# A two-layer diffusion trunk in float32: one float32 matmul per product in place of three float32r matmuls

## The chip, the cores and the metric

The kernel runs on one core of one Trainium2 chip. The metric is the device time of one execution in microseconds (us); lower is better. Such a core has a matrix engine (TensorE, PE in the profile; its weight loads stand apart as PEld), a vector engine (VectorE, DVE), an activation engine (ScalarE, ACT), GpSimd (POOL) and a queue that starts transfers (SyncE, SP). TensorE reads two operands from on-chip memory, a stationary one (`lhsT`, "the weights" of one matmul) and a moving one (`rhs`), and adds its results up in PSUM banks.

## The reference

One step of a trunk of two layers on 384 tokens: 128 of a prompt, 256 of a sample. The same weights serve both. Everything is float32.

```python
def _layer(x, cond, lw, rope, ctx):
    mod = (silu(cond) @ lw['w_mod'] + lw['b_mod'])          # 9 vectors of 1024 per condition
    def pre(j, t):
        return _rmsnorm(t, lw['norm_g'][j]) * (1.0 + mod[3*j+1]) + mod[3*j]
    x = x + 0.5 * mod[2] * _swiglu(pre(0, x), ffn_in[0], ffn_out[0])     # 1024 -> 2*2816 -> 1024
    y, new_ctx = _mixer(pre(1, x), lw, rope, ctx)
    x = x + mod[5] * y
    x = x + 0.5 * mod[8] * _swiglu(pre(2, x), ffn_in[1], ffn_out[1])
    return x, new_ctx
```

The mixer multiplies its input with `w_in` (1024 x 5888), runs three branches (attention of 8 heads with 2 key heads, a gated linear recurrence of 4 heads in both directions called HGRN2, and attention within a window), multiplies each with a 512 x 1024 matrix, gates and adds them, and multiplies with `w_out` (1024 x 1024). The outputs are the tokens after a last norm, the prompt's keys and values, and the recurrence's states.

## The kernel before

Activations lie with features on the 128 partitions and the 384 tokens along the row, as eight tiles `xt[k]`. A weight matrix comes from HBM in chunks of at most 128 x 1024 float32 (512 KB), each of which holds up to eight 128 x 128 blocks. A product of one block with one activation tile is called a product here: it adds 128 out features x 384 tokens into a PSUM bank.

Each product is three matmuls (`mm3`, line 211). The type float32r is a float32 that TensorE takes with a rounded mantissa; a number is split into an upper float32r part and the rest as a lower one. `wchunk` (line 194) loads a chunk into a tile `wr` (4 buffers), casts it on ScalarE to `wh` (line 200) and subtracts that on VectorE for `wl` (line 201). `split` (line 204) does the same with activations (`ah`/`al`, `oh`/`ol`, `mh`/`ml`); `norm_tile` makes `hh`/`hl`, `residual` makes `xh`/`xl`, `key_parts` and `query_parts` the parts for the scores of attention (`kh`, `kl`, `kpr`, `kpl`, `qst`). `mm3` adds upper x upper, upper x lower and lower x upper.

The order of the work: a start in which the first modulation vectors come on TensorE (`mod_start`, with 32-column matmuls on `condS`, then four 2-column ones against `sel`); then for each layer a SwiGLU (`ffn`), the mixer, and a second SwiGLU. A SwiGLU has a first group of six out tiles with the k tiles outermost (`first_group`, 48 products), 19 pairs of out tiles of eight products each per tile (304), and eight out tiles of 22 products (176). The mixer has a first group (48), 24 products of 256 columns for the values, 40 tiles of eight (320), two token-major pieces of 24 products with 512 columns (`by_token`), the three branch matrices (96) and `w_out` (64). In layer 0 the first group of the first SwiGLU has 384 columns, the five other first groups have 386.

Attention, HGRN2 and the other modulation vectors (`mods`: tiles `wm` of 512 KB, two reductions on VectorE each, line 236) are side work, written as generators. `side.pump` is called after each chunk with the nominal time of its products and lets each generator go on by its rate. `UN` is this nominal time for one product; `ATR`, `HGR` and `MMX` set the rates. So the program text sets which side work stands between which products. A tool of the language then orders the instructions for each engine by priority; each engine runs its own in that order, and waits by semaphores.

These matmuls are plain float32 in both kernels: the sums of squares against `ones`, broadcasts against `ident`, attention's transposes and weighted sums (`weigh`), everything in `hg_head`, and the head norms of the queries in `q_norms` (line 836), which go to four groups of 32 columns of TensorE, one for each of the four query tiles:

```python
for j, x in enumerate(xs):
    sq = block("sq")
    A.activation(sq, x, AF.Square)
    mm(p[32 * j:32 * j + 32], bd32, sq, True, True)
```

Of the kernel before, what the change touches and what calls it, by code (L numbers as in the profile page):

```python
# [9 lines left out]
F32 = mybir.dt.float32  # L10
F32R = mybir.dt.float32r
# [19 lines left out]
AHEAD = 60  # L31
MMX = 320.0
NBLK = 60
NWH = 4
NWL = 4
NWR = 4
URG = 100
HGR = 2.0
ATR = 2.4
# [4 lines left out]
def tile_trunk(ctx: ExitStack, tc: tile.TileContext, ins: dict, outs: dict, depth=DEPTH):  # L44
# [63 lines left out]
    # silu(cond), features on the partitions: 32 columns, of which two count  # L108
# [30 lines left out]
    def lower_bounds():  # L139
        """softmax over the layers, cumulated, less the first"""  # L140
# [63 lines left out]
    def split(src, name):  # L204
        hi = block(name + "h", F32R)
        lo = block(name + "l", F32R)
        A.copy(hi, src)  # L207
        V.tensor_tensor(lo, src, hi, ALU.subtract)  # L208
        return hi, lo

    def mm3(out, w, x, start, stop):
        mm(out, w[0], x[0], start, False)
        mm(out, w[0], x[1], False, False)
        mm(out, w[1], x[0], False, stop)

    def wslice(c, i):
        return c[0][:, i * P:(i + 1) * P], c[1][:, i * P:(i + 1) * P]
# [21 lines left out]
    def start_tile(tag):  # L239
        return wp.tile([P, 1024], F32, tag=tag, bufs=3 if tag == "wm" else NWL, name=nm("st"))  # L240

    def mod_start_load(g):
        ws = []
        for q, tag in enumerate(("wm", "tok", "wm", "wl")):
# [36 lines left out]
    def mods(*ljs):  # L281
        """loads run one tile ahead of the sums"""
# [41 lines left out]
    def rstd_bcast(ps_cols, n, width):  # L324
        """rows of sums (token-major) -> 1/sqrt(mean + eps), small tile"""
# [8 lines left out]
    def norm_scale(state, copy=True):  # L334
        """1 / sqrt(mean + eps) of every token, on all partitions"""
# [11 lines left out]
    def norm_tile(bc, l, j, k):  # L347
        if True:
            t = block("t")
            for c, a, b in CONDS:  # L350
                V.scalar_tensor_tensor(t[:, a:b], xt[k][:, a:b], mcol(l, 3 * j + 1, k, c), bc[:, a:b],  # L351
                                       ALU.mult, ALU.mult)
            hi = block("hh", F32R)
            lo = block("hl", F32R)
            for c, a, b in CONDS:
                sh = mcol(l, 3 * j, k, c)
                A.activation(hi[:, a:b], t[:, a:b], AF.Identity, bias=sh)  # L357
                V.scalar_tensor_tensor(lo[:, a:b], t[:, a:b], sh, hi[:, a:b], ALU.add, ALU.subtract)
            return hi, lo

    def group_part(name, l, ps, xs, kp, raws=None):
        cs = [wchunk(ins[name][l, kp, e], 768, raws[2 * kp + e] if raws else None) for e in range(2)]
        for kk in range(2):
            k = 2 * kp + kk
            for e in range(2):
                for q in range(3):
                    mm3(ps[3 * e + q], wslice(cs[e], 2 * q + kk), xs[k], k == 0, k == KT - 1)
# [17 lines left out]
    def group_scale(p, bcs):  # L385
        """the scale of the norm on a product, and the products of the shifts"""
# [7 lines left out]
    def residual(state, n, ps, l, j, nxt):  # L394
# [4 lines left out]
        if nxt is not None:  # L399
            l2, j2 = nxt  # L400
            hi = block("xh", F32R, T + 2)
            lo = block("xl", F32R, T + 2)
            for c, a, b in CONDS:
                gs = mcol(l2, 3 * j2 + 1, n, c)
                A.activation(hi[:, a:b], xt[n][:, a:b], AF.Copy, scale=gs)
                V.scalar_tensor_tensor(lo[:, a:b], xt[n][:, a:b], gs, hi[:, a:b], ALU.mult, ALU.subtract)
            sh = modt[l2][:, 24 * j2 + n]
            A.copy(hi[:, T:T + 2], sh)
            V.tensor_tensor(lo[:, T:T + 2], sh, hi[:, T:T + 2], ALU.subtract)
            state["xs"].append((hi, lo))  # L410
        sumsq_add(state, xt[n])

# [1 line left out]
    def ffn(state, l, i, nxt, mhid=(), mout=(), start=None):  # L414
        acts = []

        def finish_pair(pg, pu):
# [4 lines left out]
            acts.append(split(s, "a"))  # L422
# [8 lines left out]
        else:  # L431
# [3 lines left out]
            for j in range(first):  # L435
# [5 lines left out]
                acts.append(split(tu, "a"))  # L441
        for j in range(first, FT):
            pair = []
            for w in range(2):
                c = pre.pop(0) if pre else wchunk(ins["wfi"][l, i, j, w], 1024)
                p = pside() if j == first else pmain()
                for k in range(KT):
                    mm3(p, wslice(c, k), hs[k], k == 0, k == KT - 1)
# [6 lines left out]
            if j == first:  # L455
                tm = side.add(mods(*mhid), (8 * len(mhid) + 1) / 128.0)
# [3 lines left out]
        tm = side.add(mods(*mout), (8 * len(mout) + 1) / 62.0)  # L460
        for n in range(KT):
            p = pmain()
            for q, (a, b) in enumerate(((0, 8), (8, 15), (15, 22))):
                c = wchunk(ins["wfo"][l, i, n][:, a * P:b * P], (b - a) * P)
                for k in range(a, b):
                    mm3(p, wslice(c, k - a), acts[k], k == 0, k == FT - 1)
# [7 lines left out]
    def rope(dst, src, tmp):  # L474
        """dst = src * cos + swapped(src) * sin on the sample's columns"""
# [7 lines left out]
    def key_parts(keys, kp):  # L483
        """float32r parts of the keys of both kv heads: the upper part of a head on both halves of the partitions,
        the lower part too; the prompt's keys apart"""
        res = []
        pr = block("kpr", F32R).rearrange("p (a b) -> p a b", a=3)
        pl = block("kpl", F32R).rearrange("p (a b) -> p a b", a=3)
        for g in range(2):
            kh, kl = block("kh", F32R), block("kl", F32R)  # L490
            own, oth = slice(64 * g, 64 * g + 64), slice(64 - 64 * g, 128 - 64 * g)
            for src, h, lo in ((keys, kh, kl), (kp, pr[:, g], pl[:, g])):
                A.copy(h[own], src[own])
                A.copy(h[oth], src[own])
                V.tensor_tensor(lo[own], src[own], h[own], ALU.subtract)
                V.tensor_tensor(lo[oth], src[own], h[own], ALU.subtract)
            res.append((kh, kl, pr[:, g], pl[:, g]))
        return res

    def query_parts(qt, hf):  # L500
        """[upper; lower] float32r parts of one head on the halves of the partitions"""
        st = block("qst", F32R)
        own, oth = slice(64 * hf, 64 * hf + 64), slice(64 - 64 * hf, 128 - 64 * hf)
        A.copy(st[own], qt[own])
        V.tensor_tensor(st[oth], qt[own], st[own], ALU.subtract)
        return st

    def scores(l, win, j, hf, st, ks, rq):
        hidx = 4 * hf + j
        kh, kl, ph, pl = ks[hf]  # L510
# [45 lines left out]
    def weigh(pts, vs):  # L556
        """the heads of a pair take turns: each has one half of the columns of TensorE"""
# [9 lines left out]
    def attn_task(specs):  # L567
        """specs: (layer, win, q tiles, key parts, scales of q, values, result); heads overlap by one"""
        work = [(sp, j, hf) for sp in specs for j in range(4) for hf in range(2)]
        parts = {}  # L570

        def prepare(w):
# [604 lines left out]
```

## Time and profile before

| | before |
|---|---|
| median of 3 runs | 1965.35 us (1963.71 to 1965.65) |
| profiled execution, first to last instruction (span) | 1962.9 us |
| what lies around it (median less span) | 2.45 us |
| TensorE busy | 1943.3 us, 11958 matmul records |
| VectorE busy | 1445.4 us |
| ScalarE busy | 903.6 us |
| moved by DMA | 303.81 MB, 155 GB/s over the span |

The profiled execution's own total is not listed apart; its span is what its rows add up to. A record is one instruction that the profiler saw on an engine. Matmul records overlap: the engine streams the columns of the next one while the results of the last one still drain, and the end of a record is modelled. So what one matmul costs in a stream is the distance from start to start, not the duration of its record.

### The profile page before, as it was taken

Reading aid. Unit: us, or ns where it says so; the run is one execution under the profiler, and the core shown is the slowest. Engines: PE = TensorE matmul, PEld = TensorE weight load, DVE = VectorE, ACT = ScalarE, POOL = GpSimd, SP = SyncE. Lnnn points to the kernel's source line nnn. Section 1 sums busy time; section 2 is a strip of 40 time slices with the busy share of each in tenths; the row PEclk is TensorE's granted clock in tenths of the full one; section 3 lists DMA queues with packets and bytes.
Section 4 is the critical chain, followed back from the end, with each engine's and each line's share of the span. In section 5 each row is a group of like instructions: output and inputs, shape, how many; then the busy total and the mean of one; then the engine's idle time right before and its main releaser. Section 6 shows DMA issues by size and latency. Waiting matters only on the chain.

```text
span 1962.9 us, 31192 instructions
## 1 busy us (share of the span) xinstructions
PE 1943.3 (99%) x11958; PEld 1878.0 (96%) x11958; DVE 1445.4 (74%) x2945; ACT 903.6 (46%) x1764; POOL 13.2 (1%) x28
## 2 busy tenths in 40 slices
PE   7999999999999999999999999999999999999998
PEld 4999999998999999999999999998989999999998
DVE  4697876878888689866579869588878867765433
ACT  4433334665555454333353333356655545533331
POOL 0000000000000000000000000000000000000000
PEclk8999999999999999999999999999999999999999
DMA  7775653422334347655447657443213334444441
GB/s 277 247 254 193 226 195 121 134 87 76 113 114 135 124 139 235 216 190 177 141 157 238 222 184 251 124 132 108 86 55 114 97 104 145 151 161 156 122 126 64
DMA packets 94517, 303.81 MB, mean 155 GB/s; under 512 B 11936, under 2 KB 16416, under 8 KB 94368
## 3 DMA queue, kind: packets, MB, share of 16 engines
q1 hardware_dynamic: 93600, 300.25, 46.7%
q8 instruction: 94, 1.54, 0.3%
q0 software_dynamic: 768, 1.57, 0.2%
q14 instruction: 55, 0.45, 0.1%
HBM read 298.63 MB, written 3.15 MB: 154 GB/s over the span
## 4 chain that ended last, share of the span: by engine, by line
PE 98%; DMA 1%; DVE 0%; SPq 0%; ACT 0%; issue 0%; DVEq 0%
PE pm L82 83%; PE ps L82 14%; PE ps L548 1%; DMA st<-in_wst 0%; DMA wr<-in_wfg 0%; SPq L88 0%; DVE y L1068 0%; PE ps L549 0%; PE ps L775 0%; PE ps L715 0%; PE ps L714 0%; ACT wh L200 0%; DVE x L397 0%; PE ps L842 0%; ACT sq L303 0%
## 5 line engine op out<-in xcount | busy, mean ns | idle before, releaser
L200 ACT CAST wh<-wr 128x1024 fp32r<-128x1024 f32 (+3 forms) x460 | 444.6, 967 | 802.7 <-PE pm L82 414.1
L201 DVE TENSOR_TENSOR wl<-wr,wh 128x1024 fp32r<-128x1024 f32 (+3 forms) x460 | 513.8, 1119 | 210.8 <-ACT wh L200 205.3
L82 PE MATMUL pm<-hh,wh 128*128 128x384 f32 x1816 | 617.4, 340 | 0.0
L82 PE MATMUL pm<-hl,wh 128*128 128x384 f32 x1816 | 613.8, 338 | 0.0
L82 PE MATMUL pm<-hh,wl 128*128 128x384 f32 x1816 | 611.7, 337 | 0.0
L236 DVE CUSTOM_DVE_ANT_0 junk<-wm,cond 128x1024 bf16<-128x1024 f32 x256 | 312.7, 1222 | 55.7 <-DMA wm<-in_wmod 49.9
L82 PEld LDWEIGHTS pm<-hh,wh 128*128 128x128 f32 x1816 | 340.8, 188 | 6.8 <-issue 3.1
L82 PEld LDWEIGHTS pm<-hl,wh 128*128 128x128 f32 x1816 | 341.1, 188 | 1.9 <-DVE t L351 0.8
L82 PEld LDWEIGHTS pm<-hh,wl 128*128 128x128 f32 x1816 | 341.5, 188 | 1.4 <-issue 1.4
L82 PE MATMUL pm<-al,wh 128*128 128x384 f32 x704 | 237.3, 337 | 0.0
L82 PE MATMUL pm<-ah,wl 128*128 128x384 f32 x704 | 237.0, 337 | 0.0
L82 PE MATMUL pm<-ah,wh 128*128 128x384 f32 x704 | 237.0, 337 | 0.0
L82 PEld LDWEIGHTS pm<-al,wh 128*128 128x128 f32 x704 | 132.3, 188 | 0.0
L82 PEld LDWEIGHTS pm<-ah,wl 128*128 128x128 f32 x704 | 132.2, 188 | 0.0
L82 PEld LDWEIGHTS pm<-ah,wh 128*128 128x128 f32 x704 | 132.1, 188 | 0.0
L397 DVE SCALAR_TENSOR_TENSOR x<-pm,modt,x 128x128 f32<-128x128 f32 x96 | 35.5, 412 | 56.7 <-PE pm L82 56.6
L421 DVE TENSOR_TENSOR silu<-pm,silu 128x384 f32<-128x384 f32 x73 | 40.5, 555 | 48.0 <-PE pm L82 47.6
L207 ACT CAST ah<-silu 128x384 fp32r<-128x384 f32 x79 | 40.4, 512 | 35.4 <-DVE silu L421 35.0
L357 ACT ACTIVATE hh<-t,modt 128x128 fp32r<-128x128 f32 x96 | 42.4, 454 | 29.8 <-DVE t L351 29.6
L82 PE MATMUL pm<-oh,wh 128*128 128x384 f32 x128 | 46.2, 361 | 0.0
L208 DVE TENSOR_TENSOR al<-silu,ah 128x384 fp32r<-128x384 f32 x79 | 43.5, 551 | 1.5 <-ACT ah L207 1.5
L351 DVE SCALAR_TENSOR_TENSOR t<-x,modt,bcs 128x128 f32<-128x128 f32 x96 | 37.1, 412 | 10.1 <-ACT bcs L344 10.0
(306 smaller groups left out, 2737.4 us busy)
## 6 DMA issues: line engine op xcount, KB each, us to landing
wr<-in_wfi SPq DMA_DIRECT2D x152, 512.0 KB, 3.8
wm<-in_wmod SPq DMA_DIRECT2D x128, 512.0 KB, 4.6
wr<-in_win SPq DMA_DIRECT2D x80, 512.0 KB, 3.7
wr<-in_wfo SPq DMA_DIRECT2D x64, 448.0 KB, 3.4
wr<-in_wfo SPq DMA_DIRECT2D x32, 512.0 KB, 3.6
wr<-in_wfg SPq DMA_DIRECT2D x32, 384.0 KB, 3.1
wr<-in_wbr SPq DMA_DIRECT2D x48, 256.0 KB, 2.6
st<-in_wst SPq DMA_DIRECT2D x16, 512.0 KB, 7.0
```

The costliest lines, as they stand in the source:

```text
L82: PE.matmul(out, lhsT=lhsT, rhs=rhs, start=start, stop=stop)
L200: A.copy(hi, raw)
L201: V.tensor_tensor(lo, raw, hi, ALU.subtract)
L207: A.copy(hi, src)
L208: V.tensor_tensor(lo, src, hi, ALU.subtract)
L236: V.tensor_tensor_reduce(junk, w, cond[c], 1.0, 0.0, ALU.mult, ALU.add, accum_out=modt[l][:, n, c:c + 1])
L351: V.scalar_tensor_tensor(t[:, a:b], xt[k][:, a:b], mcol(l, 3 * j + 1, k, c), bc[:, a:b], ALU.mult, ALU.mult)
L357: A.activation(hi[:, a:b], t[:, a:b], AF.Identity, bias=sh)
L397: V.scalar_tensor_tensor(xt[n][:, a:b], ps[:, a:b], mcol(l, j, n, c), xt[n][:, a:b], ALU.mult, ALU.add)
L421: V.tensor_tensor(s, pu, s, ALU.mult)
L548: PE.transpose(dst, pb[1 + b][:, kt * P:(kt + 1) * P], ident)
```

## The change

`mm3` is gone: each product is one `mm` on the float32 tile `wr` as it came from HBM and on float32 activations. `wchunk` only loads; the casts, the subtractions, `split`, `key_parts` and `query_parts` are gone with their tiles. Behind `weigh` one copy from PSUM remains (`o`). The scores of a head are products on the 64 partitions of that head, three per head in place of six. The pool sizes are `NWR` = 14 buffers for `wr` (4 before, beside 4 each for `wh` and `wl`) and `NBLK` = 52 (60). The nominal time and the rates of the side work change, and modulation vectors 6 and 7 (in layer 1 also 5) move from the SwiGLU to the mixer.

```diff
-AHEAD = 60
-MMX = 320.0
-NBLK = 60
-NWH = 4
-NWL = 4
-NWR = 4
+MMX = 150.0
+NBLK = 52
+NWR = 14
-HGR = 2.0
-ATR = 2.4
+HGR = 1.5
+ATR = 1.55
...
-    def wchunk(src, cols, raw=None):
-        if raw is None:
-            raw = wraw(src, cols)
-        hi = wp.tile([P, 1024], F32R, tag="wh", bufs=NWH, name=nm("wh"))[:, :cols]
-        lo = wp.tile([P, 1024], F32R, tag="wl", bufs=NWL, name=nm("wl"))[:, :cols]
-        with tc.high_priority(offset=AHEAD):
-            A.copy(hi, raw)
-            V.tensor_tensor(lo, raw, hi, ALU.subtract)
-        return hi, lo
...
-    def mm3(out, w, x, start, stop):
-        mm(out, w[0], x[0], start, False)
-        mm(out, w[0], x[1], False, False)
-        mm(out, w[1], x[0], False, stop)
+    def wchunk(src, cols):
+        return wraw(src, cols)
...
-    UN = 3 * 0.163
+    UN = 0.34
...
-                    mm3(p, wslice(c, k), hs[k], k == 0, k == KT - 1)
+                    mm(p, wslice(c, k), hs[k], k == 0, k == KT - 1)
...
-                tm = side.add(mods(*mhid), (8 * len(mhid) + 1) / 128.0)
+                tm = side.add(mods(*mhid), (8 * len(mhid) + 1) / 95.0)
...
-        for b, (h, lo) in ((1, (kh, kl)), (0, (ph, pl)), (2, (kh, kl))):
-            mm(regs[b], st[:, b * P:(b + 1) * P], h, True, False)
-            mm(regs[b], st[:, b * P:(b + 1) * P], lo, False, True)
+        for b, ks in ((1, keys), (0, kp), (2, keys)):
+            mm(regs[b], qt[own, b * P:(b + 1) * P], ks[own], True, True)
...
-        st = ffn(st, l, 0, (l, 1), [(l, 4), (l, 3), (l, 2 if l == 0 else 5)],
-                 [(l, 7), (l, 6)], (ps, hs) if l == 0 else None)
-        st = mixer(st, l, [(l, 5)] if l == 0 else [])
-        st = ffn(st, l, 1, None if end else (l + 1, 0), [(l, 8)] + ([] if end else [(l + 1, 1), (l + 1, 0)]),
-                 [] if end else [(l + 1, 2)])
+        st = ffn(st, l, 0, (l, 1), [(l, 2), (l, 4), (l, 3)], [], (ps, hs) if l == 0 else None)
+        st = mixer(st, l, [(l, 5), (l, 7), (l, 6)])
+        st = ffn(st, l, 1, None if end else (l + 1, 0), [(l, 8)] + ([] if end else [(l + 1, 1), (l + 1, 0)]), [])
```

Three places show what stands in a row on an engine. First, TensorE at the start of the second half of layer 0's first SwiGLU, before (a row is line, instruction, out<-in, and the weights' columns x the moving columns; `pm` is a PSUM bank):

```order
L82 MATMUL pm_2055<-ah_584,wh_2058 128x384
L82 MATMUL pm_2055<-al_585,wh_2058 128x384
L82 MATMUL pm_2055<-ah_584,wl_2059 128x384
L82 MATMUL pm_2055<-ah_591,wh_2058 128x384
L82 MATMUL pm_2055<-al_592,wh_2058 128x384
L82 MATMUL pm_2055<-ah_591,wl_2059 128x384
```

and now (`silu` is the activation that was split into `ah` and `al`):

```order
L78 MATMUL pm_1047<-silu_413,wr_1048 128x384
L78 MATMUL pm_1047<-silu_416,wr_1048 128x384
L78 MATMUL pm_1047<-silu_419,wr_1048 128x384
L78 MATMUL pm_1047<-silu_440,wr_1048 128x384
L78 MATMUL pm_1047<-silu_471,wr_1048 128x384
```

One instruction of the program stands for each product where three stood; the sequence of products is the same.

Second, TensorE at the scores of the first attention head, before (`qst` holds both parts of the query on the two halves of the partitions):

```order
L82 MATMUL ps_3681<-kh_3631,qst_3651 128x384
L82 MATMUL ps_3681<-kl_3632,qst_3651 128x384
L82 MATMUL ps_3681<-kpr_3629,qst_3651 128x128
L82 MATMUL ps_3681<-kpl_3630,qst_3651 128x128
L82 MATMUL ps_3682<-kh_3631,qst_3651 128x384
L82 MATMUL ps_3682<-kl_3632,qst_3651 128x384
```

and now (`keysA` and `qk` are keys, `gs` the query tile):

```order
L78 MATMUL ps_1743<-keysA_1356,gs_1496 128x384
L78 MATMUL ps_1743<-qk_1529,gs_1496 128x128
L78 MATMUL ps_1744<-keysA_1356,gs_1496 128x384
```

The matmuls against the lower parts of the keys have gone.

Third, the transfer queue (SP) in layer 0's mixer, in the tiles that feed the gates and the branch matrices, before:

```order
L93 DMA wm_5127<-in_wmod 128x1024
L88 DMA wr_5458<-in_win 128x1024
L88 DMA wr_5529<-in_win 128x1024
L88 DMA wr_5585<-in_win 128x1024
L88 DMA wr_5662<-in_win 128x1024
L88 DMA wr_5739<-in_wbr 128x512
```

and now:

```order
L84 DMA wr_2828<-in_win 128x1024
L84 DMA wr_2885<-in_wbr 128x512
L89 DMA wm_2276<-in_wmod 128x1024
L84 DMA wr_2887<-in_wbr 128x512
L84 DMA wr_2949<-in_wbr 128x512
L89 DMA wm_2371<-in_wmod 128x1024
```

The loads of modulation tiles (`wm`) stand closer between the weight loads of the mixer.

## Rows read from the trace of the kernel before

**Rows 1.** The page's part 1: busy us (share of the span), instructions.

```profile
span 1962.9 us, 31192 instructions
PE 1943.3 (99%) x11958; PEld 1878.0 (96%) x11958; DVE 1445.4 (74%) x2945; ACT 903.6 (46%) x1764; POOL 13.2 (1%) x28
```

**Rows 2.** The page's part 2: TensorE's busy tenths and granted clock in 40 slices.

```profile
PE   7999999999999999999999999999999999999998
...
PEclk8999999999999999999999999999999999999999
```

**Rows 3.** The page's part 4: shares of the chain that ended last.

```profile
PE 98%; DMA 1%; DVE 0%; SPq 0%; ACT 0%; issue 0%; DVEq 0%
```

**Rows 4.** Waits of weight loads: engine, line, whom for, us in total, times, longest.

```profile
PEld pm L82 <- ACT hh L357: 2.6, 2, 1.8
...
PEld pm L82 <- DVE t L351: 0.8, 1, 0.8
PEld pm L82 <- DVE wl L201: 0.8, 1, 0.8
```

**Rows 5.** Stretches: from:to, length, busy us (records) per engine, PEclk, DMA share, GB/s.

```profile
100.00:200.00 100.00, 100.00 (x571) 100.00 (x570) 86.19 (x133) 35.33 (x48) 0.00 (x0) 1.00 0.66 220
...
344.00:714.00 370.00, 370.00 (x2567) 347.73 (x2566) 304.11 (x759) 213.29 (x514) 6.57 (x12) 1.00 0.36 113
1300.00:1671.00 371.00, 370.94 (x2573) 349.07 (x2572) 288.32 (x727) 213.58 (x515) 6.43 (x12) 1.00 0.32 102
```

**Rows 6.** Groups by line and form: x count | busy us, mean ns of one | idle.

```profile
L82 PE MATMUL pm<-hh,wh 128*128 128x384 f32 x1816 | 617.4, 340 | 0.0
...
L82 PE MATMUL ps<-sq,c_bd 128*32 128x384 f32 x16 | 1.7, 498 | 0.0
```

**Rows 7.** Time order, TensorE, layer 1's query norms: start, us, form, x count.

```profile
1314.61 0.53 PE L82 MATMUL ps<-sq,c_bd 128*32 128x384 f32 x4
```

**Rows 8.** The same, a little later.

```profile
1314.95 0.51 PE L82 MATMUL ps<-sq,c_bd 128*32 128x384 f32 x4
```

**Rows 9.** Time order, TensorE, start: two products on two column groups, first records.

```profile
24.88 0.62 PE L82 MATMUL ps<-st,condS 128*32 128x512 f32 x2
```

**Rows 10.** The same two products, second records.

```profile
25.33 0.60 PE L82 MATMUL ps<-st,condS 128*32 128x512 f32 x2
```

**Rows 11.** Time order, TensorE: four products of 2 columns against `sel`, and what follows.

```profile
28.73 1.05 PE L82 MATMUL ps<-c_sel,row 128*128 128x2 f32 x8
29.64 0.43 PE L82 MATMUL ps<-hh,wl 128*128 128x384 f32 x1
```

**Rows 12.** Time order, TensorE: two products of 128 columns in HGRN2, and what follows.

```profile
533.93 0.61 PE L82 MATMUL ps<-whi,am 128*128 128x128 f32 x4
534.38 0.28 PE L82 MATMUL ps<-s,qaf 128*128 128x128 f32 x1
```

**Rows 13.** Time order, TensorE: one head's six score matmuls, first of the next head's.

```profile
1336.79 0.34 PE L82 MATMUL ps<-kh,qst 128*128 128x384 f32 x1
...
1337.14 0.22 PE L82 MATMUL ps<-kpr,qst 128*128 128x128 f32 x1
...
1337.71 0.33 PE L82 MATMUL ps<-kh,qst 128*128 128x384 f32 x1
```

**Rows 14.** The page's part 5: the two splits of weights and the modulation reductions.

```profile
L200 ACT CAST wh<-wr 128x1024 fp32r<-128x1024 f32 (+3 forms) x460 | 444.6, 967 | 802.7 <-PE pm L82 414.1
L201 DVE TENSOR_TENSOR wl<-wr,wh 128x1024 fp32r<-128x1024 f32 (+3 forms) x460 | 513.8, 1119 | 210.8 <-ACT wh L200 205.3
...
L236 DVE CUSTOM_DVE_ANT_0 junk<-wm,cond 128x1024 bf16<-128x1024 f32 x256 | 312.7, 1222 | 55.7 <-DMA wm<-in_wmod 49.9
```

More of the change, by code (lines that the diff above doesn't have):

```diff
@@ L10 @@
 F32 = mybir.dt.float32
-F32R = mybir.dt.float32r
 BF16 = mybir.dt.bfloat16
@@ L192, in wraw @@
         return raw
[L194 to L214 removed]
+    def wchunk(src, cols):
+        return wraw(src, cols)
     def wslice(c, i):
[L217 to L219 removed]
+        return c[:, i * P:(i + 1) * P]
+    UN = 0.34
     def urgent():
@@ L239, in start_tile @@
     def start_tile(tag):
-        return wp.tile([P, 1024], F32, tag=tag, bufs=3 if tag == "wm" else NWL, name=nm("st"))
+        return wp.tile([P, 1024], F32, tag=tag, bufs=3 if tag == "wm" else NWR, name=nm("st"))
     def mod_start_load(g):
         ws = []
-        for q, tag in enumerate(("wm", "tok", "wm", "wl")):
+        for q, tag in enumerate(("wm", "tok", "wm", "wr")):
             if tag == "tok":
@@ L347, in norm_tile @@
     def norm_tile(bc, l, j, k):
[L348 to L359, printed above, removed]
+        t = block("t")
+        for c, a, b in CONDS:
+            V.scalar_tensor_tensor(t[:, a:b], xt[k][:, a:b], mcol(l, 3 * j + 1, k, c), bc[:, a:b],
+                                   ALU.mult, ALU.mult)
+        for c, a, b in CONDS:
+            A.activation(t[:, a:b], t[:, a:b], AF.Identity, bias=mcol(l, 3 * j, k, c))
+        return t
     def group_part(name, l, ps, xs, kp, raws=None):
-        cs = [wchunk(ins[name][l, kp, e], 768, raws[2 * kp + e] if raws else None) for e in range(2)]
+        cs = raws[2 * kp:2 * kp + 2] if raws else [wchunk(ins[name][l, kp, e], 768) for e in range(2)]
         for kk in range(2):
@@ L400, in residual @@
             l2, j2 = nxt
-            hi = block("xh", F32R, T + 2)
-            lo = block("xl", F32R, T + 2)
+            xs = block("xs", cols=T + 2)
             for c, a, b in CONDS:
[L404 to L410, printed above, removed]
+                A.activation(xs[:, a:b], xt[n][:, a:b], AF.Copy, scale=mcol(l2, 3 * j2 + 1, n, c))
+            V.tensor_copy(xs[:, T:T + 2], modt[l2][:, 24 * j2 + n])
+            state["xs"].append(xs)
         sumsq_add(state, xt[n])
@@ L421, in finish_pair @@
                 V.tensor_tensor(s, pu, s, ALU.mult)
-            acts.append(split(s, "a"))
+            acts.append(s)
         first = 3
@@ L440, in ffn @@
                     V.scalar_tensor_tensor(tu[:, a:b], tu[:, a:b], bu[:, c:c + 1], tg[:, a:b], ALU.add, ALU.mult)
-                acts.append(split(tu, "a"))
+                acts.append(tu)
         for j in range(first, FT):
@@ L459, in ffn @@
         st = new_sum(nxt is None)
-        tm = side.add(mods(*mout), (8 * len(mout) + 1) / 62.0)
+        tm = side.add(mods(*mout), (8 * len(mout) + 1) / 40.0)
         for n in range(KT):
@@ L480, in rope, with scores @@
         V.tensor_tensor(dst, tmp, sh, ALU.add)
[L483 to L508, printed above, removed]
+    def scores(l, win, j, hf, qt, keys, kp, rq):
         hidx = 4 * hf + j
-        kh, kl, ph, pl = ks[hf]
+        own = slice(64 * hf, 64 * hf + 64)
         s0 = pside(512)
@@ L569, in attn_task @@
         work = [(sp, j, hf) for sp in specs for j in range(4) for hf in range(2)]
-        parts = {}
-        def prepare(w):
-            if w < len(work):
-                sp, j, hf = work[w]
-                ks = key_parts(*sp[3]) if j + hf == 0 else parts[w - 1][1]
-                parts[w] = (query_parts(sp[2][j], hf), ks)
         pend = None
         pts = []
-        prepare(0)
-        yield
         ready = None
@@ L586, in attn_task @@
             if w < len(work):
-                (l, win, qts, kk, rqs, vs, dest), j, hf = work[w]
-                st, ks = parts[w]
-                prepare(w + 1)
-                pb = scores(l, win, j, hf, st, ks, rqs[j])
+                (l, win, qts, (keys, kp), rqs, vs, dest), j, hf = work[w]
+                pb = scores(l, win, j, hf, qts[j], keys, kp, rqs[j])
                 yield
@@ L593, in attn_task @@
                 (sp, j, hf), p0 = ready
-                sp[6][j] = split(weigh(p0, sp[5]), "o")
+                o = block("o")
+                A.copy(o, weigh(p0, sp[5]))
+                sp[6][j] = o
                 ready = None
@@ L777, in hg_task @@
                 ot = gated(hd + 1)
-            hi, lo = block("ogh", F32R), block("ogl", F32R)
-            A.activation(hi, p, AF.Copy, scale=hgg[:, l:l + 1])
-            V.scalar_tensor_tensor(lo, p, hgg[:, l:l + 1], hi, ALU.mult, ALU.subtract)
-            dest[hd] = (hi, lo)
+            og = block("og")
+            A.activation(og, p, AF.Copy, scale=hgg[:, l:l + 1])
+            dest[hd] = og
             yield
@@ L894, in prepare @@
                 yield
-        tP = side.add(prepare(), 1 / 2.0)
+        tP = side.add(prepare(), 1 / 1.5)
         tm = side.add(mods(*mmix), (8 * len(mmix) + 1) / MMX)
@@ L903, in mixer @@
                 c, kk = pre[k // 4], k % 4
-                w = (c[0][:, kk * 256:(kk + 1) * 256], c[1][:, kk * 256:(kk + 1) * 256])
-                hj = (hs[k][0][:, j * P:(j + 1) * P], hs[k][1][:, j * P:(j + 1) * P])
-                mm(pv[j], hj[0], w[0], k == 0, False)
-                mm(pv[j], hj[0], w[1], False, False)
-                mm(pv[j], hj[1], w[0], False, k == KT - 1)
-            side.pump(24 * 0.109)
+                mm(pv[j], hs[k][:, j * P:(j + 1) * P], c[:, kk * 256:(kk + 1) * 256], k == 0, k == KT - 1)
+            side.pump(8 * 2 / 3 * UN)
         vt = []
@@ L935, in by_token @@
                     k = 2 * q + kk
-                    w = (c[0][:, kk * 512:(kk + 1) * 512], c[1][:, kk * 512:(kk + 1) * 512])
                     for j in range(3):
-                        hj = (hs[k][0][:, j * P:(j + 1) * P], hs[k][1][:, j * P:(j + 1) * P])
-                        mm(ph[j], hj[0], w[0], k == 0, False)
-                        mm(ph[j], hj[0], w[1], False, False)
-                        mm(ph[j], hj[1], w[0], False, k == KT - 1)
-                side.pump(6 * 3 * 0.216)
+                        mm(ph[j], hs[k][:, j * P:(j + 1) * P], c[:, kk * 512:(kk + 1) * 512], k == 0, k == KT - 1)
+                side.pump(8 * UN)
             t = blk.tile([P, 3, 512], F32, tag="tok", bufs=2, name=nm(name))
@@ L1009, in mixer @@
                 V.tensor_tensor(mg[n], mg[n], gb[n], ALU.add)
-                ms[n] = split(mg[n], "m")
+                ms[n] = mg[n]
         st = new_sum()
```

10 lines of the change are left out of this document (5 added, 5 removed).

## The prediction

> **What bounds the kernel now.** The page's busy shares come first [rows 1]: TensorE is busy 99% of a span of 1962.9 us, VectorE 74%, ScalarE 46%. A high share of TensorE alone proves little, since matmul records overlap, so the second look is at the slices and at the chain of waits: only the first slice has a digit under 8, the granted clock is at its upper level (2.4 GHz) but for the ends [rows 2], and 98% of the chain that ended last is TensorE [rows 3]. Third, the waits: what the splitting of operands still costs TensorE is 2.6 + 0.8 + 0.8 = 4.2 us in the whole run [rows 4], although the two weight splits take 444.6 us of ScalarE and 513.8 us of VectorE [rows 14]. They run beside TensorE. So the time is a sum over TensorE's matmuls, and the question is what one float32 product costs against three float32r ones.
>
> **The price of a product before.** In 100 us of the first SwiGLU there are 571 matmul records, all with 384 columns, with TensorE busy throughout [rows 5]: 175.1 ns each, 3 x 175.1 = 525 ns per product. A float32r matmul is one record: the upper x upper group of normed tiles has 1816 [rows 6], which is what the loops issue.
>
> **The price of a product after.** No row has a float32 product of 384 columns with 128 columns of weights, so it is bounded by the nearest rows, those of `q_norms`. Its loop issues four products per layer, eight in all; the trace has 16 records [rows 6]. A float32 matmul is therefore two records. In layer 1 the first four start together at 1314.61, and four more at 1314.95 [rows 7, 8]. The four products use four different column groups and run side by side, so the two sets of four are the first and the second record of each product. The distance between the sets is 1314.95 - 1314.61 = 0.34 us from start to start; by ends it is (1314.95 + 0.51) - (1314.61 + 0.53) = 0.32 us. 384 columns at 2.4 GHz are 160 ns, so each record streams its columns twice. That the groups run side by side, and don't share one stream, is seen in the start: two products on only two column groups, 512 columns, need 25.33 + 0.60 - (24.88 + 0.62) = 0.43 us per set of records [rows 9, 10], and 2 x 512 / 2.4 = 427 ns. With half as many products at once a set still takes two passes, so the second pass is not the price of sharing. The record's mean duration says the same: 498 ns against 340 ns for a float32r one with as many columns [rows 6], 158 ns more, one more pass. Two records of two passes are four passes: 4 x 160 = 640 ns bare, 2 x 320 to 2 x 340 ns by those rows.
>
> Does the weight load add to it? Four products of 2 moving columns, eight records, take 29.64 - 28.73 = 0.91 us, 114 ns each [rows 11]; that is loading 128 columns, since two columns stream in no time. Two products of 128 columns take 534.38 - 533.93 = 0.45 us for four records, 112 ns each [rows 12], although each also streams for about 107 ns (two passes of 128 columns). So load and stream overlap, and behind 320 ns of streaming a load is hidden. The other end is a pass that costs as much as a float32r one, which needs 175 ns where 160 would do: 4 x 175 = 700 ns. I take 650 ns, near the rows of plain float32, because those are the same instruction and show no such surplus; the surplus belongs to rows of another type. 640 and 700 are kept as the ends.
>
> A rule stands beside this. The Trainium skill ("FP8 and Floating Point Precision", TensorE Precision Notes) gives true FP32 four passes, and "TensorE: Matmul & The Clock Gate" (Back-to-back issue gap) gives a warm pass N / 2.4 + 2.5 ns, 162.5 ns for 384 columns. By it three float32r passes would be 487.5 ns and a float32 product 650 ns. The trace agrees with the four passes and not with the first figure (175 measured), and the measured one decides: by the pages alone a product would cost 162 ns more and all of them +541 us, by the rows 125 ns and +416 us.
>
> **The sum.** From the loops: 384 columns: 4 x (304 + 176) in the SwiGLUs, 48 in the first group, 2 x (320 + 96 + 64) in the mixers, 2928 products; 386 columns: 5 x 48 = 240; 512: 96; 256: 48. Both prices go with the columns, so in products of 384 columns this is 2928 + 241 + 128 + 32 = 3329. Each costs 650 - 525 = 125 ns more: +416 us. With 640 ns it is +383 us, with 700 ns +583 us.
>
> Scores: a head's six matmuls take 1337.71 - 1336.79 = 0.92 us [rows 13]. Afterwards it is two products of 384 (1.30) and one of 128 (two records of 0.112): 1.52 us. 32 heads: +0.60 x 32 = +19 us (+18 to +23).
>
> What goes: the waits on split operands, 4.2 us [rows 4]. A gain of up to 10 us is possible, if switches from one type to the other also get cheaper. I take -5.
>
> The casts and subtractions go, 958 us of ScalarE and VectorE [rows 14], and are counted at nothing: TensorE hides them today, and a slower TensorE hides the rest even better. Nothing else gets late next, as each of these engines loses work while the span grows.
>
> The modulation tiles that move: the mixer of layer 0 gets 24 in place of 8, layer 1's 24 in place of none. Each is a transfer of 512 KB and two reductions of 1.22 us [rows 14]: 39 us and 59 us of VectorE. VectorE is busy 304 of 370 us in the first mixer and 288 of 371 us in the second [rows 5], but splits go from there too, and the mixer itself grows to some 450 us; priced at nothing. If that cover were gone, 98 us would show. Against that stands that the first mixer already holds eight such tiles and takes 370 us for 2567 records, the second none and 371 us for 2573 [rows 5]. The `wm` buffers are shared with attention's weights, and a `wm` load that waits for one holds up the weight loads behind it on SP and the matmuls behind those; 14 chunks of `wr` stand ready for that, at 8 x 0.65 = 5.2 us each. The transfers, 220 GB/s in the busiest of the stretches shown [rows 5], spread over a longer time.
>
> The smaller `UN` is a planner's number, not a duration. Per chunk of eight products it hands 8 x 0.34 / 1.55 = 1.75 steps to attention, where 8 x 0.489 / 2.4 = 1.63 were handed before; and a chunk now lasts 5.2 us and not 4.2. The chains of attention get more time per step, not less.
>
> Sum: +416 + 19 - 5 = +430 us on a span of 1962.9 us, 2393 us, and with 2.45 us around it **2395 us**. The median of the runs shown is span plus those 2.45 us, so the two bases agree. The case's own bounds: 1965 + 383 + 18 - 10 = 2356 and 1965 + 583 + 23 = 2571.
>
> **The rivals.** *Faster: two passes per product.* The four column groups could share what feeds the array, so that a record with all 128 columns of weights streams only once. The rows at 128 columns can't refute it, since the load sets their 112 ns [rows 11, 12]. A product would then be two records at 175, 350 ns: 3329 x (350 - 525) = -583 us, with scores at about 0.82 us per head -3 us, -5 us of waits: 1374 us. VectorE would then have to fit its mixer work into two thirds of the time, so 1370 to 1450. It decides from a product price under 525 ns. Against it: two groups and four groups show the same time per column [rows 7 to 10], which sharing would not give.
>
> *Much slower: the loads are not hidden.* If a float32 record with full weights had to wait for its own load, it would be 325 + 112 = 437 ns, 874 per product: 3329 x 349 = +1162 us, about 3150 us with the scores. Against it, load and stream overlap at 128 columns [rows 11, 12].
>
> *The side work becomes the bound.* If the moved modulation held up the mixers, up to 98 us would come on top: 2493 us. Against it: neither mixer is longer by its tiles now [rows 5].
>
> That the change doesn't do what it says is out: the rows in the order above have one float32 instruction per product.
>
> **How the numbers follow.** The forecast, with the price between 640 and 700 ns, has 0.86; the side work's delay 0.06; the faster rival 0.05; exposed loads 0.03. The range leaves out the faster rival, the exposed loads, the uppermost part of the forecast's own (700 ns belongs to the other type's rows) and the side work's upper end with it: 2356 to 2530 us. Against a bound of 0.2%, about what a measurement can tell from no change: faster 0.05, same 0.01, slower 0.94.
>
> **What would show it.** TensorE's records for products go from 9936 to 2 x 3312 = 6624, with 320 to 350 ns from start to start where it was 175; TensorE stays near 99% and its share of the chain near 98%; VectorE loses at least the 514 us of line 201. A start-to-start of 175 means the faster rival, of about 437 the exposed load. The prediction is wrong if TensorE shows idle time in the mixers, or if the records of a product are not two.

## The result and the profile after

| | before | after |
|---|---|---|
| median | 1964.9 us (4 runs, 1963.71 to 1965.65) | 2390.32 us (4 runs, 2390.0 to 2391.24) |
| span of the profiled execution | 1962.9 us | 2387.9 us |

The kernel is 1.2167 times as long (95% interval 1.2149 to 1.2184), 425.4 us by the medians and 425.0 us by the spans. The forecast was 2395 us, with a range of 2356 to 2530.

The page of the changed kernel, with the busy times, TensorE's slices and granted clock, and the chain that ended last:

```profile
span 2387.9 us, 22594 instructions
...
PE 2369.0 (99%) x8646; PEld 1395.7 (58%) x8646; DVE 829.5 (35%) x2117; ACT 402.4 (17%) x1096; POOL 13.1 (1%) x28
...
PE   8999999999999999999999999999999999999998
PEld 4555556555566555555555555565556665555555
...
PEclk9999999999999999999999999999999999999999
...
PE 99%; DVE 0%; DMA 0%; ACT 0%; issue 0%; SPq 0%; DVEq 0%
```

TensorE bounds the kernel as before [rows 1 to 3], with 3312 records fewer. The share to look at beside it is PEld: weight loads are busy 58% where it was 96%, since each now stands behind a stream twice as long. VectorE went from 74% to 35% and ScalarE from 46% to 17%, and none of that shows as a gain in the time.

The stretch that answers to the first of [rows 5] (from:to, length, busy us and records of PE, PEld, DVE, ACT and POOL, granted clock, DMA share, GB/s), and the groups that answer to [rows 6]:

```profile
100.00:200.00 100.00, 100.00 (x311) 58.90 (x310) 41.51 (x74) 4.91 (x10) 0.00 (x0) 1.00 0.50 176
```

```profile
L78 PE MATMUL pm<-t,wr 128*128 128x384 f32 x3632 | 1193.1, 487 | 0.0
L78 PE MATMUL pm<-silu,wr 128*128 128x384 f32 x1264 | 411.7, 486 | 0.0
```

311 records in 100 us are 322 ns each, where 571 were 175 ns [rows 5]. `t,wr` has 3632 records for 1816 products of the program (there were 1816 of `hh,wh`): two per product, so 644 ns (2 x 322) where three float32r matmuls were 525 ns. The mean duration of a record, 487 ns, is again far longer than its share of the stream.

### The profile page after: what moved, and what is told of

It reads as the page before. It is cut to its first block, busy times and chain, and to the rows that moved or that the text cites. A ratio compares the mean times of both kernels' runs of the same rounds, so it can differ in the third digit from the quotient of the medians.

```text
span 2387.9 us, 22594 instructions
## 1 busy us (share of the span) xinstructions
PE 2369.0 (99%) x8646; PEld 1395.7 (58%) x8646; DVE 829.5 (35%) x2117; ACT 402.4 (17%) x1096; POOL 13.1 (1%) x28
## 4 chain that ended last, share of the span: by engine, by line
PE 99%; DVE 0%; DMA 0%; ACT 0%; issue 0%; SPq 0%; DVEq 0%
PE pm L78 84%; PE ps L78 14%; PE ps L490 1%; DMA st<-in_wst 0%; DVE y L988 0%; PE ps L491 0%; PE ps L706 0%; DVE sq L290 0%; DVE sq L293 0%; PE ps L645 0%; PE ps L646 0%; SPq L84 0%; DVE x L370 0%; PE ps L772 0%; ACT row L240 0%
## 5 line engine op out<-in xcount | busy, mean ns | idle before, releaser
L78 PE MATMUL pm<-t,wr 128*128 128x384 f32 x3632 | 1193.1, 487 | 0.0
L78 PEld LDWEIGHTS pm<-t,wr 128*128 128x128 f32 x3632 | 683.3, 190 | 473.6 <-issue 13.2
L78 PE MATMUL pm<-silu,wr 128*128 128x384 f32 x1264 | 411.7, 486 | 0.0
L78 PEld LDWEIGHTS pm<-silu,wr 128*128 128x128 f32 x1264 | 240.2, 190 | 167.5
L78 PE MATMUL pm<-o,wr 128*128 128x384 f32 x256 | 89.3, 496 | 0.0
L78 PE MATMUL pm<-wr,t 128*128 128x512 f32 x192 | 85.7, 596 | 0.0
L78 PE MATMUL pm<-xs,wr 128*128 128x386 f32 x240 | 85.3, 487 | 0.0
L78 PE MATMUL ps<-xs,wr 128*128 128x386 f32 x240 | 84.5, 487 | 0.0
L78 PE MATMUL pm<-gate,wr 128*128 128x384 f32 x256 | 82.9, 486 | 0.0
L78 PE MATMUL ps<-t,wr 128*128 128x384 f32 x176 | 59.2, 488 | 0.0
```

What stands on the lines that cost most here:

```text
L78: PE.matmul(out, lhsT=lhsT, rhs=rhs, start=start, stop=stop)
```

## Experiments

The price theory says: TensorE's matmuls are the time, a product costs 644 ns in place of 525, and whatever else the change does is covered. Against it stand theories in which other parts of the change hold a share: the splits that went, the modulation tiles that moved, the buffers, or the mere mass of the stream. In the expectations, e-numbers are the runs below. Times are compared with the kernel before on the same chip (1964.2 to 1964.9 us in the three groups of runs).

### The splits put back beside the float32 matmuls (e1)

```diff
-NWR = 14
+NWR = 10
...
-    def wchunk(src, cols):
-        return wraw(src, cols)
+    def wchunk(src, cols, raw=None):
+        if raw is None:
+            raw = wraw(src, cols)
+        hi = wp.tile([P, 1024], F32R, tag="wh", bufs=2, name=nm("wh"))[:, :cols]
+        lo = wp.tile([P, 1024], F32R, tag="wl", bufs=2, name=nm("wl"))[:, :cols]
+        with tc.high_priority(offset=AHEAD):
+            A.copy(hi, raw)
+            V.tensor_tensor(lo, raw, hi, ALU.subtract)
+        return raw
...
```

> The changed kernel, in which every weight chunk is still cast on ScalarE and subtracted on VectorE as before, into two float32r tiles that no matmul reads (and 10 buffers for the chunks in place of 14, for room). If TensorE's products set the time and the splits lie beside them, they cost nothing: 2387 to 2395 us, as the changed kernel's 2390. If the splits took time from the path before, so that their removal gave something back that the slower products ate, their return costs it: over 2400 us.

Measured: 2393.31 us (ratio 1.2181, 1.2163 to 1.2199). The groups of the splits (mean ns of one, idle before):

```profile
L199 DVE TENSOR_TENSOR wl<-wr,wh 128x1024 fp32r<-128x1024 f32 (+3 forms) x460 | 514.9, 1121 | 786.2 <-ACT wh L198 785.0
L198 ACT CAST wh<-wr 128x1024 fp32r<-128x1024 f32 (+3 forms) x460 | 442.3, 963 | 1045.1 <-DMA wr<-in_wfi 419.7 <-DMA wr<-in_wfo 306.9 <-DMA wr<-in_win 78.2
```

515 us of VectorE and 442 us of ScalarE, as much as before [rows 14], cost about 3 us. The two intervals of the ratio overlap, but all four runs (2392.06 to 2394.48 us) lie above all four of the changed kernel (2390.0 to 2391.24 us), so a small price is likely there; whether it is the splits' or that of four buffers fewer was not separated. The run has a limit: no matmul reads these parts, so it shows that the work on the two engines costs next to nothing, and not what TensorE would pay if it had to wait for the parts. For the kernel before, that is the 4.2 us of [rows 4].

### The modulation back in the SwiGLUs (e2)

```diff
-        st = mixer(st, l, [(l, 5), (l, 7), (l, 6)])
+        st = mixer(st, l, [(l, 5)] if l == 0 else [])
```

and the lists of the two `ffn` calls as before.

> The changed kernel with the modulation vectors where they stood before (6 and 7 in the SwiGLU's second half, 5 in layer 1's SwiGLU, vector 2 of the next layer in the second SwiGLU's second half). If the move is covered by TensorE: 2386 to 2394 us. If part of the 425 us is the mixers held up by the moved tiles, the mixers get shorter: 2290 to 2380 us.

Measured: 2390.2 us (1.2165, 1.2147 to 1.2183), the same within the scatter of the runs (2389.59 to 2390.43 us). The move is worth nothing, either way.

### Four buffers for the weights (e8)

```diff
-NWR = 14
+NWR = 4
```

> The changed kernel with 4 buffers for the weight chunks in place of 14. If a chunk's 5.2 us of products cover its transfer (3.5 us to landing), no more than four are needed: 2388 to 2396 us. If the moved modulation loads hold up the queue and the fourteen buffers hide that, TensorE shows idle time in the mixers: over 2400 us.

Measured: 2392.22 us (1.2176, 1.2158 to 1.2194). Ten buffers fewer make about 2 us at most.

### One part alone: the second halves of the SwiGLUs (e4)

```diff
-            acts.append(split(s, "a"))
+            acts.append(s)
...
-                c = wchunk(ins["wfo"][l, i, n][:, a * P:b * P], (b - a) * P)
+                c = wraw(ins["wfo"][l, i, n][:, a * P:b * P], (b - a) * P)
...
-                    mm3(p, wslice(c, k - a), acts[k], k == 0, k == FT - 1)
+                    mm(p, c[:, (k - a) * P:(k - a + 1) * P], acts[k], k == 0, k == FT - 1)
```

> The kernel before, in which only the second halves of the four SwiGLUs (4 x 176 products) are one float32 matmul each, with neither their weights nor their activations split. If each product costs 645 - 525 = 120 ns more wherever it stands: 704 x 0.12 = +84 us, 2044 to 2054 us, and the four halves take 114 us each where they took 92. If the price came from the whole stream (a clock, contention with the other engines, the missing prefetch), the part alone would not show its share: under 2030 or over 2065 us.

Measured: 2049.72 us, +85.1 (1.0431, 1.0414 to 1.0449). A stretch inside the first such half:

```profile
230.00:310.00 80.00, 80.00 (x249) 47.12 (x248) 39.72 (x83) 8.56 (x22) 0.00 (x0) 1.00 0.57 181
```

80 us for 249 records are 321 ns. 704 products at +119 ns are 84 us. The price is a matter of each product, not of the whole stream.

### Two float32r matmuls per product: the price that the faster rival gave (e6)

```diff
-            V.tensor_tensor(lo, raw, hi, ALU.subtract)
...
-        mm(out, w[0], x[1], False, False)
-        mm(out, w[1], x[0], False, stop)
+        mm(out, w[0], x[1], False, stop)
...
```

> The kernel before with two float32r matmuls per product, upper x upper and upper weights x lower activations; the third one is left out, with the subtraction that makes the lower parts of the weights. A product then costs 350 ns, the price that the faster rival gave a float32 product. If TensorE's matmuls alone set the time: 3329 x 0.175 = 583 us less, 1378 to 1390 us. If at this price something else becomes the bound, as that rival supposed (VectorE in the mixers, or the transfers in the SwiGLUs' first halves, which would need some 300 GB/s there with four buffers): 1400 to 1480 us, with idle time of TensorE in those stretches.

Measured: 1454.94 us (0.7402, 0.739 to 0.7415), 510 us less and not 583. The page's busy times, two waits of TensorE (us in total, times, longest), its mean clock, and the stretch that holds layer 0's mixer:

```profile
span 1458.0 us, 23917 instructions
...
PE 1399.3 (96%) x8646; PEld 1310.7 (90%) x8646; DVE 965.1 (66%) x2485; ACT 891.6 (61%) x1764; POOL 13.2 (1%) x28
```

```profile
PE pm L82 <- ACT silu L417: 14.4, 3, 4.9
PE pm L82 <- ACT gate L968: 6.2, 6, 1.8
```

```profile
core 0: 1458.0 us, clock 0.985
```

```profile
256.00:548.00 292.00, 282.84 (x1996) 251.08 (x1995) 223.54 (x674) 209.60 (x513) 6.54 (x12) 1.00 0.43 141
```

At 350 ns per product TensorE is idle 1458.0 - 1399.3 = 58.7 us, 39 more than before [rows 1], 9 of them in this mixer. Three waits of nearly 5 us each are for `silu` behind the first group of a SwiGLU. They end with ScalarE, but ScalarE itself had waited. In the order of time around the first of them, on VectorE, ScalarE and TensorE:

```profile
582.74 1.22 DVE L233 CUSTOM_DVE_ANT_0 junk<-wm,cond 128x1024 bf16<-128x1024 f32 x1
583.88 0.55 DVE L418 TENSOR_TENSOR silu<-ps,silu 128x384 f32<-128x384 f32 x1
```

```profile
584.46 0.51 ACT L205 CAST ah<-silu 128x384 fp32r<-128x384 f32 x1 [1.86 <-DVE silu L418]
584.88 0.48 ACT L417 ACTIVATE silu<-pm 128x384 f32<-128x384 f32 x1
```

```profile
585.42 0.44 PE L82 MATMUL pm<-hh,wh 128*128 128x384 f32 x1 [4.74 <-ACT silu L417]
```

```profile
575.00:592.00 17.00, 12.26 (x62) 11.94 (x61) 16.96 (x34) 8.41 (x15) 0.00 (x0) 0.90 0.76 269
```

The `silu` that TensorE waits for stands on ScalarE behind a cast, which waits for a product on VectorE, which stands behind the reductions of modulation tiles (`junk`). VectorE is busy 16.96 of these 17 us. The second wait looks the same (16.97 of 17 us from 770 to 787 us). At the third VectorE is not full (9.18 of 17 us from 1280 to 1297 us), but the product again stands behind two reductions, the first of which had waited for its tile:

```profile
1285.38 1.23 DVE L233 CUSTOM_DVE_ANT_0 junk<-wm,cond 128x1024 bf16<-128x1024 f32 x1 [1.85 <-DMA wm<-in_wmod]
```

The mean clock is 0.985, where the profiled runs of before and after have 0.996 and 0.997. Part of that lies behind these waits: TensorE had been idle 4.74 us, and then worked at the lower level (1.2 GHz) for some 3 us, until the upper one was granted again (from:to, length, busy us and records of PE, granted clock, DMA share, GB/s):

```profile
586.00:588.00 2.00, 2.00 (x8) 0.50 0.43 174
588.00:590.00 2.00, 2.00 (x10) 0.71 0.79 262
590.00:592.00 2.00, 2.00 (x14) 1.00 0.00 0
```

So side work on VectorE, which costs nothing at 525 or 644 ns per product, shows at 350 in this kernel. It is not the changed kernel at that price: it still casts every weight chunk on ScalarE, splits the activations, and has four buffers for `wr`. The transfers of weight chunks (`wr`) were not named by any of the longest waits of TensorE, though all transfers together reached 374 GB/s in one stretch:

```profile
80.00:100.00 20.00, 20.00 (x116) 20.00 (x115) 18.94 (x36) 9.89 (x14) 0.00 (x0) 1.00 0.99 374
```

The 16 engines are 99% busy there, and TensorE still takes 116 records in 20 us, about 175 ns each, counting the records that reach over the edges.

### Four float32r matmuls per product (e9)

```diff
-        mm(out, w[1], x[0], False, stop)
+        mm(out, w[1], x[0], False, False)
+        mm(out, w[1], x[1], False, stop)
...
```

> The kernel before with a fourth float32r matmul per product, lower weights x lower activations: four passes per product, as many as a float32 product makes, and the splits as before. If a float32r pass costs 175 ns wherever it stands: 3329 x 175 = 583 us more, 2540 to 2556 us, some 155 us slower than float32 with its four passes of 161 ns. If four passes in a row on one product cost the same in either type, and the surplus of a float32r pass came from the order of the three terms or from the splits beside them: 2360 to 2400 us.

Measured: 2541.1 us, +577 (1.2937, 1.2918 to 1.2956).

```profile
100.00:200.00 100.00, 100.00 (x572) 100.00 (x571) 66.89 (x99) 26.47 (x36) 0.00 (x0) 1.00 0.51 166
```

572 records in 100 us are 175 ns each. Four passes of float32r are 4 x 175 ns and 151 us slower than the four passes of plain float32. This is the upper end of the forecast's price, 700 ns, made real: it belongs to float32r and not to float32.

### float16 in place of float32r (e7)

```diff
-F32R = mybir.dt.float32r
+F32R = mybir.dt.float16
```

> The kernel before with float16 in place of float32r for all the parts: three matmuls per product as before, the parts have fewer bits. If the 15 ns by which a float32r pass of 384 columns is longer than 160 ns belong to 4-byte operands that stream one column per cycle, they go: 3329 x 3 x about 12 ns = 120 us less, 1835 to 1855 us. If they belong to any dense stream of matmuls with a new weight load each: 1955 to 1967 us.

Measured: 1850.85 us, -114 (0.9423, 0.9409 to 0.9437). A stretch of the first SwiGLU:

```profile
100.00:180.00 80.00, 80.00 (x495) 48.19 (x493) 74.99 (x117) 28.15 (x39) 0.00 (x0) 1.00 0.71 237
```

80 us for 495 records are 162 ns in place of 175. PEld falls to 60% of this stretch, so the weight load got shorter too; the run changes both, the width of the streamed operand and the load. Which of the two gives the 13 ns is taken up in the last section. This is the fastest of the versions that keep all three terms, 6% under the kernel before, with parts of fewer bits.

### The scores alone (e3), and on all partitions (e5, e10)

```diff
-        for b, (h, lo) in ((1, (kh, kl)), (0, (ph, pl)), (2, (kh, kl))):
-            mm(regs[b], st[:, b * P:(b + 1) * P], h, True, False)
-            mm(regs[b], st[:, b * P:(b + 1) * P], lo, False, True)
+        for b, ks in ((1, keys), (0, kp), (2, keys)):
+            mm(regs[b], qt[own, b * P:(b + 1) * P], ks[own], True, True)
```

> The kernel before, in which only the scores of attention are float32 products on 64 partitions, without the parts of keys and queries. By the price of a product (645 ns with 384 columns, 224 ns with 128, against 0.92 us for a head's six matmuls) 32 heads cost 19 us more: 1981 to 1989 us. If the parts of keys and queries on ScalarE and VectorE stood in attention's chain and cost more than that, it is level or faster: 1955 to 1970 us.

Measured: 1994.25 us, +29.7 (1.015, 1.0135 to 1.0165), 10 us more than the price theory had. In the order of time (start, us, form, count):

```profile
407.35 0.34 PE L82 MATMUL pm<-hh,wl 128*128 128x384 f32 x1
407.62 0.91 PE L82 MATMUL ps<-keysA,gs 64*128 64x384 f32 x2
408.37 0.38 PE L82 MATMUL ps<-qk,gs 64*128 64x128 f32 x2
408.59 0.81 PE L82 MATMUL ps<-keysA,gs 64*128 64x384 f32 x2
409.32 0.44 PE L82 MATMUL pm<-hh,wh 128*128 128x384 f32 x1
409.60 0.34 PE L82 MATMUL pm<-hl,wh 128*128 128x384 f32 x1
```

A head is six records, as reckoned. But it starts 0.27 us behind a float32r pass of 0.175, its first two records take 0.75 us where two of 0.322 would take 0.64, its last two 0.73 us until the product behind it starts, and the next product starts 0.28 us later. That is 0.10 + 0.11 + 0.09 + 0.10 us more, about 0.4 in all. The weight loads in these places (PEld) show what happens:

```profile
407.62 0.29 PEld L82 LDWEIGHTS ps<-keysA,gs 64*128 64x128 f32 x2 [0.24 <-issue]
...
409.32 0.19 PEld L82 LDWEIGHTS pm<-hh,wh 128*128 128x128 f32 x1 [0.55 <-issue]
```

The first load of the head and the first load behind it begin together with their own matmuls (407.62 and 409.32), some 0.09 us after the stream before has ended. So on the way in and on the way out the load is not hidden, and about 0.1 us of it shows. The next run takes away one suspect, the change between weights of 64 and of 128 rows (against e3; the moving operand gets 128 rows too):

```diff
+            for src, out in ((keys, res[0]), (kp, res[1])):
+                for g in range(2):
+                    t = block("pad")[:, :src.shape[1]]
+                    own, oth = slice(64 * g, 64 * g + 64), slice(64 - 64 * g, 128 - 64 * g)
+                    V.memset(t[oth], 0.0)
+                    A.copy(t[own], src[own])
...
-            mm(regs[b], qt[own, b * P:(b + 1) * P], ks[own], True, True)
+            mm(regs[b], qt[:, b * P:(b + 1) * P], ks, True, True)
```

> The float32 scores in the kernel before once more (e3, 1994.25 us), now on all 128 partitions: the keys of each head stand in a tile of their own whose other half is zero, so each score matmul has weights of 128 rows like the products around it. In e3 the first record of a head waits about 100 ns longer than its 323 ns, and the first product behind a head about 90 ns. If that is the change between weights of 64 and of 128 rows, both go: 32 heads x 0.19 us = 6 us less, 1986 to 1990 us. If it comes from the change between float32 and float32r or from the semaphore that a head's first matmul waits for, nothing goes: 1992 to 1997 us.

Measured: 1982.75 us, 11.5 us less than e3 (1.0092, 1.0077 to 1.0107), more than expected.

```profile
405.80 0.34 PE L82 MATMUL pm<-hh,wl 128*128 128x384 f32 x1
405.98 1.67 PE L82 MATMUL ps<-pad,gs 128*128 128x384 f32 x6
407.19 0.63 PE L82 MATMUL pm<-hh,wh 128*128 128x384 f32 x1
407.66 0.34 PE L82 MATMUL pm<-hl,wh 128*128 128x384 f32 x1
```

```profile
405.80 1.23 PEld L82 LDWEIGHTS ps<-pad,gs 128*128 128x128 f32 x6
```

With full weights the loads of the head begin at 405.80, beside the pass before it, and the head starts 0.18 us behind that pass. The second product behind it starts at 407.66, so that 407.66 - 0.175 - 405.98 = 1.51 us are the head's own; in e3 it is 409.60 - 0.175 - (407.35 + 0.175) = 1.90. The expectation had counted two of the four delays. The six records are what the prediction said, 1.52 us, and the kernel with padded float32 scores is 17.9 us slower than the kernel before, where +19 was reckoned. The other 0.4 us per head are the change of the rows.

> The changed kernel with the scores on all 128 partitions, the other half of each head's keys zero, as in e5. If the change between weights of 64 and of 128 rows costs the changed kernel what it cost the kernel before (e3 less e5: 11.5 us): 2376 to 2382 us. If that was a matter of the change between float32 and float32r, which the changed kernel does not have, nothing goes: 2388 to 2392 us.

Measured: 2380.32 us (1.2119, 1.2099 to 1.214), 10.0 us less than the changed kernel. Its rows of a head, without and with the padding (two kernels, each in its own fence; the last row of the first one is the second record behind the head, singled out):

```profile
485.46 0.27 PE L491 MATMUL ps<-c_ident,p 128*128 128x128 f32 x1
485.66 0.91 PE L78 MATMUL ps<-keysA,gs 64*128 64x384 f32 x2
486.41 0.38 PE L78 MATMUL ps<-qk,gs 64*128 64x128 f32 x2
486.63 0.81 PE L78 MATMUL ps<-keysA,gs 64*128 64x384 f32 x2
487.37 0.91 PE L78 MATMUL pm<-t,wr 128*128 128x384 f32 x2
...
487.80 0.49 PE L78 MATMUL pm<-t,wr 128*128 128x384 f32 x1
```

```profile
484.69 0.27 PE L491 MATMUL ps<-c_ident,p 128*128 128x128 f32 x1
484.80 1.68 PE L78 MATMUL ps<-pad,gs 128*128 128x384 f32 x6
486.31 5.32 PE L78 MATMUL pm<-t,wr 128*128 128x384 f32 x16
```

0.20 us from the last transpose to the first score against 0.11, and 1.71 us for the head against 1.51; the first record behind the head then takes 0.43 us (487.37 to 487.80) where one of 0.322 is due. Together that is the same 0.4 us per head. So the delay does not need a change of type: it is there between float32 and float32. For 32 heads it would be about 12.5 us; that 10.0 came back and not all of it was not taken apart.

## Why the prediction was right

**What bounds the kernel.** Right. That TensorE's sum is the time was read from 4.2 us of waits on split operands [rows 4], and e1, e2, e4 and e9 hold it up: what TensorE does adds up within some 1% (+85 where +84 was reckoned, +577 where +583), and what the others do shows in some 3 us at most. It stops being so at a price of 350 ns (e6).

**Four passes.** Right. The step that carried the forecast was to read two records per product out of 16 records for 8 products, and two passes per record out of the distance between two sets on four column groups [rows 6 to 8]. Products with all 128 columns of weights behave the same. The sharing of a stream, on which the faster rival rested, is refuted by the 322 ns.

**The price.** 650 ns was taken, 644 measured: 3329 x 6 ns = 20 us too much. The rows of plain float32 were the right end; e9 shows that the other end, 700 ns, is what float32r would cost.

**The loads.** Hidden in the products, as read from [rows 11, 12]: 322 ns is two passes of 160 ns and 2 ns. They are not hidden where the rows of the weights change, which is the next term.

**The scores.** The term was mis-sized: +19 reckoned, +29.7 measured alone (e3). The records were right (e5, +17.9 with all rows); that a stream of 64-row weights inside one of 128-row weights costs some 0.4 us on the way in and out was not in the sum. [Rows 13] could not show it, since before the scores too had weights of 128 rows. But the trace of before has a relative of it, at the products with weights of 32 columns in the query norms:

```profile
1314.35 0.33 PE L82 MATMUL pm<-hh,wl 128*128 128x384 f32 x1
```

They start at 1314.61 [rows 7], 0.26 us behind this pass of 0.175, where 0.18 would be dense.

**The waits.** -5 us was taken. With 3329 x (644 - 525) = +396 us and +30 us for the scores, 426 us are explained of 425.0, so about -1 us is left for the waits that went and everything else. That remainder is smaller than what the reading of a record's length decides (1 ns per record is 2 x 3329 ns = 6.7 us) and is not settled here.

**What was counted at nothing.** Splits (e1, about 3 us with four buffers fewer), moved modulation (e2, none), buffers (e8, about 2 us): right each time, by the named cover. The rates of the side work, `UN` and `NBLK` were not tried alone; the remainder above is all that the sum leaves for them.

So the forecast was 5 us off because two terms were, +20 and -10, and the waits by some 4. Its parts were less exact than its sum: that it came so close is in part luck.

**The rivals.** The faster one was also asked for its number: with two float32r matmuls per product, 350 ns, the kernel before takes 1455 us, not 1374, just above the 1370 to 1450 that it gave. For the changed kernel at that price this is only a stand-in, since it keeps the casts, the split activations and the four buffers. The rival's mechanism for the rest, VectorE that no longer fits its work in, is what e6 shows, but in another place: the three long waits lie behind the first group of a SwiGLU, where VectorE has modulation in front of the product that is needed, and not in the mixers. Of the 78 us between the span of 1458 and the 1380 of the sum (1962.9 - 583), 39 are more idle time of TensorE; how the others divide between the lower clock and stalls that the records hide was not taken apart. The slower rivals have no support: a product takes 644 ns and not 874, and moving the modulation back (e2) changes nothing.

## What to carry to other kernels

Where one engine's stream is the time, price the new instruction first, by rows of the same instruction however small, and count its records against the program's: here eight products with sixteen records decided between 30% faster and 22% slower. "One in place of three" says nothing until the passes are counted, and 958 us less work on two other engines is worth next to nothing under a full stream (e1, about 3 us). Look also at what a term changes in its neighbours' operands: a change in the rows of the weights costs on the way in and out, and no price per record has that in it. Padding with zeros to 128 rows took most of it back here (e5, e10).

## What the runs showed of the hardware

A pass of 384 columns takes three different times in dense streams at the upper clock level: 175 ns in float32r (571 records in 100 us, and 572 in e9), 162 ns in float16 (495 in 80 us), and 161 ns in float32, where a record of two passes takes 322. The surplus of a float32r pass over its bare 160 ns was not isolated by a run of its own, but it goes with the columns. In a dense stretch of the kernel before with 512 columns, 35 records start in 8.15 us (the 36th that is counted is the tail of the one before):

```profile
371.88:380.03 8.15, 8.15 (x36) 1.00 0.47 147
```

That is 233 ns where 213 would be bare: 20 ns more, and 15 ns more with 384 columns. The load is the same 128 columns in both, so a fixed price of the load does not explain it. That float32 shows only 2 ns per record says less, because a record of two passes leaves a load twice the time.

Where the weights change between 64 and 128 rows, the load of the first new weights did not begin before the stream of the old ones had ended. This cost about 0.4 us for each head's scores, half on the way in and half on the way out, in a float32r stream (e3 to e5, 11.5 us) and in a float32 one (10.0 us).
